# A two-layer encoder trunk on one core: packed first transfer, held transfers, an earlier first norm and one smaller store

## The chip, the core and the metric

The kernel runs on one core of a Trainium2 chip. Its engines are PE (matrix products), ACT and DVE (elementwise work), POOL (a few small operations) and SP (which only issues transfers). The metric is the device time of one execution in microseconds, so less is better. Every engine works through its own instructions strictly in order; a tile framework puts waits on semaphores where one engine needs another's result.

## What is computed

The input is 256 tokens of 2048 features; 16 learned tokens are put in front, so there are L = 272 columns. Layer 0 is differential attention with 8 heads, layer 1 a causal pooling mixer. All products are float32 products made of three products of rounded halves (high x high, high x low, low x high).

```python
def rms_norm(x, g):
    y = xf * lax.rsqrt(jnp.mean(xf * xf, axis=-1, keepdims=True) + RMS_EPS)
    return (y * g.astype(jnp.float32)).astype(x.dtype)
...
for i in range(DEPTH):
    hn = rms_norm(h, pre_norm_g[i])
    if i % N_MIXERS == 0:
        y = diff_attention_mixer(hn, attn_w_in[j], attn_w_out[j], ...)
    else:
        y = pool_mixer(hn, pool_w_in[j], pool_w_group[j], pool_scale[j], pool_w_out[j])
    h = h + rms_norm(y, post_norm_g[i])
return h[:, N_META:]
```

## The kernel before

Activations lie transposed: 2048 features are 16 **feature tiles** (numbered 0 to 15 here) of 128 partitions by 272 tokens. A **chunk** is 128 output columns of a weight matrix for all 16 feature tiles (128 x 2048 numbers, 1 MB). Some 120 chunks stream through the core: SP loads one into `raw` (two buffers), ACT rounds it into `hi`, DVE subtracts to get `lo` (`split`, lines 97 and 98), and PE makes 48 products with it (`mm3`, lines 121 to 123).

**The front** is different, since nothing is there to compute on. The array `first` holds, for every feature tile, the 272 tokens of x and the weights of the first four chunks, 784 numbers per partition. It comes in eleven transfers on SP's queue into `pk`: of tile 0 the first 400 columns (line 209) and the rest (line 210), tiles 1, 2 and 3 alone, then pairs (line 212). The small parameters (gains and such, 70 columns) come in a transfer of their own on ACT's queue into `sp` (line 140). PE first makes products of ones (`busy`, line 136) with nothing but time as their result.

The loop over the feature tiles k does, per tile: ACT rounds the weights (line 236, "cast") and writes x times its gain, rounded (line 240, "scale"); DVE subtracts for the low halves of the weights (line 237) and of x (line 241, `xl`); PE makes 12 products (lines 245 to 247: four chunks, three products each); ACT squares x in place (`square0`, line 230). A square of tile k must wait until DVE has read x of that tile in line 241.

The 16 squared tiles are added up on DVE by halving (`fold`, line 107, and line 261), to `sq0`. The **first norm** (`Norm`, lines 166 to 192) then takes: small products of `sq0` with ones on PE (line 174), mean plus epsilon on DVE (line 179), the power -1/2 on POOL (line 180), a spread onto the columns of a matrix on DVE (line 190), and a product with ones on PE (line 191) that gives every partition the factors. They are needed only after the projections (rows of `rp`, lines 270 and 271), so PE can run ahead of them. Before, the fifth chunk (`pq4`, all 48 products) runs first; the norm's small products and the spread stand within the sixth chunk (`pq5`).

Tiles and pools decide which buffer waits for which; the order within each engine is set by a scheduler from the order in the source and the `issue_after` notes. Behind the front, PE runs chunk after chunk to the end, where the last block of 128 tokens is scaled and stored (`out_store`): the first 512 columns by way of PE and ACT's queue, the rest by DVE in slices, each stored by SP (lines 806 and 808).

Of the kernel before, what the change touches and what calls it, by code (L numbers as in the profile page):

```python
# [43 lines left out]
def trunk(ctx: ExitStack, tc: tile.TileContext, first, hT, xt, small, gpost1, rope, w_in, w_out, p_in, p_grp, p_out, out):  # L44
# [95 lines left out]
    act.dma_start(sp, small)  # L140
    rp = const.tile([P, 2, L], F32, name="rp")
    ident = const.tile([P, P], F32, name="ident")
# [3 lines left out]
    ones = const.tile([P, P], F32, name="ones")  # L146
    pool.memset(ones, 1.0)
    warm = const.tile([P, 1], F32, name="warm")
    act.square(warm, ones[:, 0:1])
# [49 lines left out]
    busy(6)  # L199
# [6 lines left out]
    pk = xp.tile([P, KT, L + NF * P], F32, name="pk")  # L206
# [25 lines left out]
    for k in range(KT):  # L232
        hi, lw = fhi[:, k], flo[k // 8][:, k % 8]
        for i, n in ((0, 1), (1, NF - 1)) if k == 0 else ((0, NF),):
# [3 lines left out]
            if i == 0:  # L238
                g = sp[:, C_PRE0 + k:C_PRE0 + k + 1]
# [32 lines left out]
    run_part(NF + 1, 12, 4)  # L272
# [8 lines left out]

    lp = const.tile([P, 2], F32, name="lp")
    dve.tensor_tensor(out=lp, in0=sp[:, C_LAM:C_LAM + 2], in1=sp[:, C_LAM + 2:C_LAM + 4], op=ALU.mult)
    psl = bank("psl")
    pe.matmul(psl[:, 0:2], ones, lp, start=True, stop=True)
    le = const.tile([P, 2], F32, name="le")
    act.activation(le, psl[:, 0:2], AF.Exp)
    dve.scalar_tensor_tensor(out=lamc, in0=le[:, 0:1], scalar=LAM_INIT, in1=le[:, 1:2], op0=ALU.add, op1=ALU.subtract)
# [221 lines left out]
    for slot in range(NH * 6 + KT):  # L510
# [17 lines left out]
        if slot == NF + 2:  # L528
# [372 lines left out]
```

## Time and profile before

| what | value |
|---|---|
| median of 3 runs | 837.65 us (837.34 to 837.66) |
| profiled execution: time | 837.55 us |
| profiled execution: span, first to last instruction | 835.8 us |
| PE busy | 827.9 us (99%) |
| DVE, ACT busy | 585.4 us (70%), 437.8 us (52%) |
| share of the time to the chain that ended last | PE 98%, transfers 1% |

PE is busy nearly all the time, so what the end depends on is PE's own work and the few stretches in which PE has to wait: the first 8 us, a norm, and the last 8 us. The time of the profiled execution is 1.75 us longer than its span, and lies 0.10 us under the median of the runs.

### The profile page before, as it was taken

What the parts mean: (1) busy time and instruction counts of PE and PEld (TensorE: products, weight loads), DVE (VectorE), ACT (ScalarE), POOL (GpSimd) and SP (SyncE); (2) the same over time, 40 slices, a digit from 0 to 9 for tenths busy, and PEclk for the clock granted to TensorE, in tenths of its full rate; (3) what the DMA queues carried; (4) which work ended last, traced back from release to release, by engine and by line L of the source; (5) the groups of instructions that cost most, each with busy time, mean ns of one, the idle gap of its engine ahead of it and who ended that gap; (6) DMA issues with size and microseconds to landing.
All of it is one profiled execution on the core that took longest, in us unless ns stands there. A gap on an engine that the chain in (4) does not pass through costs nothing.

```text
span 835.8 us, 14454 instructions
## 1 busy us (share of the span) xinstructions
PE 827.9 (99%) x6060; PEld 796.5 (95%) x6060; DVE 585.4 (70%) x960; ACT 437.8 (52%) x680; POOL 3.4 (0%) x13
## 2 busy tenths in 40 slices
PE   9999999999999999999999999999999999999997
PEld 8999999999999999999999999999999888888886
DVE  6799767675868687897854644697998666685523
ACT  8646555454546465855444544654544545563422
POOL 0000000000000000000000000000000000000000
PEclk9999999999999999999999999999999999999999
DMA  9446444444444444355459744146556555545512
GB/s 356 170 151 203 154 153 157 163 164 162 160 152 152 152 151 151 134 175 197 152 193 367 280 174 151 51 162 242 184 195 263 176 191 202 178 174 206 197 51 101
DMA packets 22385, 149.35 MB, mean 179 GB/s; under 512 B 2608, under 2 KB 2992, under 8 KB 5552
## 3 DMA queue, kind: packets, MB, share of 16 engines
q1 hardware_dynamic: 22032, 148.14, 48.7%
q8 instruction: 47, 0.77, 0.4%
q10 hardware_dynamic: 288, 0.30, 0.1%
q14 instruction: 18, 0.15, 0.1%
HBM read 146.33 MB, written 2.10 MB: 178 GB/s over the span
## 4 chain that ended last, share of the span: by engine, by line
PE 98%; DMA 1%; DVE 0%; ACT 0%; issue 0%; SPq 0%; DVEq 0%; ACTq 0%
PE p L121 14%; PE p L123 14%; PE p L122 14%; PE pv L129 7%; PE py L121 4%; PE py L123 4%; PE py L122 4%; PE pu L121 4%; PE pu L122 4%; PE pu L123 4%; PE pv L130 4%; PE pz L772 4%; PE pz L770 4%; PE pz L771 3%; PE pm L129 2%; PE pq L245 1%
## 5 line engine op out<-in xcount | busy, mean ns | idle before, releaser
L98 DVE TENSOR_TENSOR lo<-raw,hi 128x2048 fp32r<-128x2048 f32 (+1 forms) x123 | 279.2, 2270 | 136.4 <-ACT hi L97 135.9
L97 ACT CAST hi<-raw 128x2048 fp32r<-128x2048 f32 (+1 forms) x123 | 232.9, 1895 | 194.0 <-PE p L122 96.2
L121 PE MATMUL p<-xs,hi 128*128 128x272 f32 x928 | 270.2, 291 | 0.0
L123 PE MATMUL p<-xs,lo 128*128 128x272 f32 x928 | 268.4, 289 | 0.0
L122 PE MATMUL p<-xs,hi 128*128 128x272 f32 x928 | 267.5, 288 | 0.0
L121 PEld LDWEIGHTS p<-xs,hi 128*128 128x128 f32 x928 | 174.8, 188 | 0.3
L122 PEld LDWEIGHTS p<-xs,hi 128*128 128x128 f32 x928 | 174.8, 188 | 0.0
L123 PEld LDWEIGHTS p<-xs,lo 128*128 128x128 f32 x928 | 174.6, 188 | 0.0
L129 PE MATMUL pv<-hs,hi 128*128 128x512 f32 x256 | 89.5, 393 | 0.0
L121 PE MATMUL py<-os,hi 128*128 128x272 f32 x256 | 74.3, 290 | 0.0
L123 PE MATMUL py<-os,lo 128*128 128x272 f32 x256 | 74.1, 289 | 0.0
L122 PE MATMUL py<-os,hi 128*128 128x272 f32 x256 | 73.7, 288 | 0.0
L130 PE MATMUL pv<-hs,lo 128*128 128x256 f32 x256 | 71.8, 280 | 0.0
L121 PE MATMUL pu<-hs,hi 128*128 128x260 f32 (+3 forms) x224 | 63.8, 285 | 0.0
L123 PE MATMUL pu<-hs,lo 128*128 128x260 f32 (+3 forms) x224 | 63.7, 285 | 0.0
L122 PE MATMUL pu<-hs,hi 128*128 128x260 f32 (+3 forms) x224 | 63.6, 284 | 0.0
L129 PEld LDWEIGHTS pv<-hs,hi 128*128 128x128 f32 x256 | 48.0, 188 | 10.9
L122 PEld LDWEIGHTS py<-os,hi 128*128 128x128 f32 x256 | 48.3, 189 | 0.0
L121 PEld LDWEIGHTS py<-os,hi 128*128 128x128 f32 x256 | 48.2, 188 | 0.0
L123 PEld LDWEIGHTS py<-os,lo 128*128 128x128 f32 x256 | 48.2, 188 | 0.0
L130 PEld LDWEIGHTS pv<-hs,lo 128*128 128x128 f32 x256 | 48.1, 188 | 0.0
L771 PE MATMUL pz<-lo,zs 128*128 128x512 f32 (+1 forms) x120 | 45.0, 375 | 0.0
(251 smaller groups left out, 1316.9 us busy)
## 6 DMA issues: line engine op xcount, KB each, us to landing
raw<-in_w_in SPq DMA_DIRECT2D x60, 1024.0 KB, 4.8
raw<-in_p_in SPq DMA_DIRECT2D x29, 1024.0 KB, 4.8
raw<-in_w_out SPq DMA_DIRECT2D x16, 1024.0 KB, 4.8
raw<-in_p_out SPq DMA_DIRECT2D x14, 1024.0 KB, 4.8
pk<-in_first SPq DMA_DIRECT2D x6, 784.0 KB, 10.8
raw<-in_p_grp SPq DMA_DIRECT2D x4, 1024.0 KB, 4.9
rawu<-in_p_in SPq DMA_DIRECT2D x3, 1024.0 KB, 5.4
h<-in_hT SPq DMA_DIRECT2D x4, 544.0 KB, 7.2
```

Of the source, the lines that this page charges most:

```text
L97: act.copy(hi[:, s], raw[i][:, s])
L98: rest[i] = dve.tensor_tensor(out=lw[:, s], in0=raw[i][:, s], in1=hi.bitcast(F32)[:, s], op=ALU.subtract)
L121: pe.matmul(o, wh, xh, start=first, stop=False)
L122: pe.matmul(o, wh, xl, start=False, stop=False)
L123: pe.matmul(o, wl, xh, start=False, stop=last)
L129: pe.matmul(ps[:, 0:2 * n], wh, x, start=first, stop=False, skip_group_check=not first)
L130: pe.matmul(ps[:, 0:n], wl, x[:, 0], start=False, stop=last)
L245: pe.matmul(o, hi[:, i], xh[:, k, :], start=k == 0, stop=False)
L770: pe.matmul(ps, zh[:, k, s], wh[:, c], start=k == 0, stop=False)
L771: pe.matmul(ps, zh[:, k, s], wl[:, c], start=False, stop=False)
L772: pe.matmul(ps, zl[:, k, s], wh[:, c], start=False, stop=k == KT - 1)
```

## The change

- The small parameters move into the first columns of `first`, so the first transfer carries 470 columns instead of 400, and ACT's small transfer is gone. POOL copies them to `sp`.
- Before the transfer of feature tile 2 is issued, POOL writes one number into its place, copied from the first transfer's data. So SP's queue waits there until the first transfer has landed and POOL has run; the later transfers stand behind it in SP's order.
- `ones` is set by DVE instead of POOL, and `busy` makes 7 products instead of 6.
- The first norm's products stand in the fifth chunk (after 8 and 13 of its 16 feature tiles); the fold of the second half of the squares goes ahead of the sixth chunk's `lo`; the attention's lambda is computed in the front; the seventh chunk's `split` comes behind the norm, the eighth's halves are made apart.
- The last store's columns 512 to 2048 go out as 256, 512, 512, 256 columns instead of 640, 512, 384.

```diff
-    sp = const.tile([P, C_END], F32, name="sp")
-    act.dma_start(sp, small)
+    ones = const.tile([P, P], F32, name="ones")
+    dve.memset(ones, 1.0)
...
-    busy(6)
+    busy(7)
...
-    nc.sync.dma_start(pk[:, 0, 0:L + P], first[:, 0, 0:L + P])
-    nc.sync.dma_start(pk[:, 0, L + P:], first[:, 0, L + P:])
-    for a, b in ((1, 2), (2, 3), (3, 4), (4, 6), (6, 8), (8, 10), (10, 12), (12, 14), (14, 16)):
-        nc.sync.dma_start(pk[:, a:b, :], first[:, a:b, :])
-    load(NF)
-    nc.sync.dma_start(rp, rope)
+    ends = [0, C_END + L + P] + [C_END + k * (L + NF * P) for k in (1, 2, 3, 4, 6, 8, 10, 12, 14, 16)]
+    for a, b in zip(ends, ends[1:]):
+        if a == ends[3]:
+
+            pool.tensor_copy(pks[:, a:a + 1], pks[:, 0:1])
+        with (tc.issue_after(held.ins) if a > ends[3] else ExitStack()):
+            held = nc.sync.dma_start(pks[:, a:b], first[:, a:b])
+    act.square(warm, ones[:, 0:1])
+    pool.tensor_copy(sp, pks[:, 0:C_END])
+    with tc.issue_after(held.ins):
+        load(NF)
+        nc.sync.dma_start(rp, rope)
...
-    split(NF + 1)
+    fold(s8[:, 8:KT], s8[:, 8])
+    t = dve.tensor_tensor(out=sq0, in0=s8[:, 0], in1=s8[:, 8], op=ALU.add)
+    with tc.issue_after(t.ins):
+        split(NF + 1)
     load(NF + 3)
-    with tc.issue_after(rest[NF + 1].ins):
-        fold(s8[:, 8:KT], s8[:, 8])
-        dve.tensor_tensor(out=sq0, in0=s8[:, 0], in1=s8[:, 8], op=ALU.add)
-    run_part(NF, 0, KT)
-    run_part(NF + 1, 0, 5)
+    run_part(NF, 0, 8)
     norm0 = Norm(sq0, "pre0", rcol0).power()
-    with tc.issue_after(norm0.vi.ins):
-        split(NF + 2)
-    run_part(NF + 1, 5, 7)
-    dve.tensor_copy(r0, norm0.spread(r0))
+    run_part(NF, 8, 5)
+    r0c = dve.tensor_copy(r0, norm0.spread(r0))
...
+    run_part(NF, 13, 3)
+    with tc.issue_after(r0c.ins):
+        split(NF + 2)
...
+    run_part(NF + 1, 0, KT)
...
-        for c in (slice(512, 1152), slice(1152, 1664), slice(1664, D)) if b else (slice(0, 512), slice(512, 1280), slice(1280, D)):
+        for c in (slice(512, 768), slice(768, 1280), slice(1280, 1792), slice(1792, D)) if b else (slice(0, 512), slice(512, 1280), slice(1280, D)):
```

What it does to the order on the engines shows at two places. On **ACT**, feature tiles 1 to 4: a row that reads fhi<-pk 128x512 is the cast of a tile, xs<-pk the scale, pk<-pk the square. Before, from the cast of tile 1 on:

```order
L236 CAST fhi<-pk 128x512
L240 ACTIVATE xs<-pk,sp 128x272
L236 CAST fhi<-pk 128x512
L240 ACTIVATE xs<-pk,sp 128x272
L230 ACTIVATE pk<-pk 128x272
L236 CAST fhi<-pk 128x512
L240 ACTIVATE xs<-pk,sp 128x272
L230 ACTIVATE pk<-pk 128x272 x2
L236 CAST fhi<-pk 128x512
```

After the change, again from the cast of tile 1 to that of tile 4:

```order
L241 CAST fhi<-pk 128x512
L245 ACTIVATE xs<-pk 128x272
L235 ACTIVATE pk<-pk 128x272
L241 CAST fhi<-pk 128x512
L245 ACTIVATE xs<-pk 128x272
L241 CAST fhi<-pk 128x512
L245 ACTIVATE xs<-pk 128x272
L235 ACTIVATE pk<-pk 128x272 x2
L241 CAST fhi<-pk 128x512
```

The square of tile 1 has moved from behind the scale of tile 2 to ahead of the cast of tile 2. PE's order moves within three tiles, too: the 12 products of tile 4 stood in threes of one kind (three of line 245, three of 246, three of 247, then the fourth chunk's), and now stand chunk by chunk, so the third of them already reads the low half `xl` of x.

On **DVE**, from the split of the fifth chunk (lo, in two halves) to the norm's factors (r), before:

```order
L222 TENSOR_TENSOR lo_127<-raw_115,hi_126 128x1024 x2
L98 TENSOR_TENSOR lo_412<-raw_118,hi_411 128x2048
L107 TENSOR_TENSOR pk<-pk 128x4x272
L107 TENSOR_TENSOR pk<-pk 128x2x272
L107 TENSOR_TENSOR pk<-pk 128x272
L261 TENSOR_TENSOR sq_99<-pk 128x272
L179 TENSOR_SCALAR v_pre_488<-rms_pre_484 128x3
L98 TENSOR_TENSOR lo_492<-raw_398,hi_491 128x2048
L190 TENSOR_SCALAR r_87<-ident,rcol_83 128x16
```

After the change:

```order
L227 TENSOR_TENSOR lo_129<-raw_117,hi_128 128x1024 x2
L107 TENSOR_TENSOR pk<-pk 128x4x272
L107 TENSOR_TENSOR pk<-pk 128x2x272
L107 TENSOR_TENSOR pk<-pk 128x272
L263 TENSOR_TENSOR sq_98<-pk 128x272
L98 TENSOR_TENSOR lo_418<-raw_120,hi_417 128x2048
L177 TENSOR_SCALAR v_pre_451<-rms_pre_447 128x3
L188 TENSOR_SCALAR r_85<-ident,rcol_81 128x16
```

The fold and `sq0` now come ahead of the sixth chunk's `lo`, which still stands ahead of the norm's first DVE step; between that step and the factors no split stands any more.

## Rows read from the trace of the kernel before

**Rows 1.** The page's first part: busy time of each engine, share of the span, instructions.
```profile
PE 827.9 (99%) x6060; PEld 796.5 (95%) x6060; DVE 585.4 (70%) x960; ACT 437.8 (52%) x680; POOL 3.4 (0%) x13
```

**Rows 2.** The waits of PE over the whole span: who waited for whom, us in total, times, longest.
```profile
PE pq L245 <- ACT xs L240: 0.8, 2, 0.6
...
PE rms_pre L191 <- DVE r L190: 0.2, 1, 0.2
```

**Rows 3.** The chain of waits in its first stretch, in order of time: start, us, what.
```profile
1.65 4.83 DMA pk<-in_first
...
6.50 0.62 ACT fhi L236
7.12 0.43 ACT xs L240
...
7.60 0.64 PE pq L245 x3
```

**Rows 4.** What the transfers moved in three stretches from the span's start; the last column is GB/s over the stretch.
```profile
0.00:3.43 3.43, 2.30 (x10) 2.30 (x11) 0.06 (x1) 1.49 (x2) 1.13 (x9) 1.00 0.45 129
0.00:5.00 5.00, 3.67 (x15) 3.38 (x16) 1.27 (x6) 2.83 (x6) 1.13 (x9) 1.00 0.58 168
0.00:6.48 6.48, 5.15 (x22) 4.86 (x23) 1.48 (x6) 3.04 (x6) 1.13 (x9) 1.00 0.68 215
```

**Rows 5.** SP's first two issues on the timeline: start, us, line.
```profile
0.74 0.38 SPq L209 DMA_DIRECT2D pk<-in_first  x1
1.17 0.42 SPq L210 DMA_DIRECT2D pk<-in_first  x1
```

**Rows 6.** Transfers by issue: KB each, us from issue to landing. The first two are those of rows 5; the third is of two issues, those of tiles 1 (1.65, in rows 3) and 2 (2.11), with their mean.
```profile
pk<-in_first SPq DMA_DIRECT2D x1, 200.0 KB, 2.7
pk<-in_first SPq DMA_DIRECT2D x1, 192.0 KB, 2.8
pk<-in_first SPq DMA_DIRECT2D x2, 392.0 KB, 5.1
```

**Rows 7.** ACT's timeline, tiles 1 to 4 of the front.
```profile
7.47 0.62 ACT L236 CAST fhi<-pk 128x512 fp32r<-128x512 f32 x1
...
8.74 0.60 ACT L236 CAST fhi<-pk 128x512 fp32r<-128x512 f32 x1
...
10.51 0.43 ACT L230 ACTIVATE pk<-pk 128x272 f32<-128x272 f32 x1 [0.42 <-DVE xs L241]
10.85 0.60 ACT L236 CAST fhi<-pk 128x512 fp32r<-128x512 f32 x1
```

**Rows 8.** DVE's timeline: the low half of x of tile 1 and of tile 4.
```profile
7.76 0.50 DVE L241 SCALAR_TENSOR_TENSOR xs<-pk,sp,xs 128x272 fp32r<-128x272 f32 x1
...
12.10 0.50 DVE L241 SCALAR_TENSOR_TENSOR xs<-pk,sp,xs 128x272 fp32r<-128x272 f32 x1
```

**Rows 9.** PE's timeline: the first product of tile 5, the first of the fifth chunk, the first norm's small products and the second product behind them, the last product ahead of the spread, the spread, and the first product of the seventh chunk.
```profile
13.72 0.29 PE L245 MATMUL pq<-xs,fhi 128*128 128x272 f32 x1
...
30.27 0.28 PE L121 MATMUL pq<-xs,hi 128*128 128x272 f32 x1
...
38.22 0.72 PE L174 MATMUL rms_pre<-ones,sq 128*128 128x1 f32 x6
...
39.01 0.29 PE L122 MATMUL pq<-xs,hi 128*128 128x272 f32 x1
...
41.91 0.29 PE L121 MATMUL pq<-xs,hi 128*128 128x272 f32 x1
42.37 0.73 PE L191 MATMUL rms_pre<-r,ones 128*128 128x272 f32 x2 [0.17 <-DVE r L190]
...
44.07 0.37 PE L121 MATMUL p<-xs,hi 128*128 128x272 f32 x1
```

**Rows 10.** DVE's timeline between the front and the norm: `lo` of the fifth chunk, of the sixth, the fold, `sq0`.
```profile
26.66 2.36 DVE L222 TENSOR_TENSOR lo<-raw,hi 128x1024 fp32r<-128x1024 f32 x2
29.73 2.29 DVE L98 TENSOR_TENSOR lo<-raw,hi 128x2048 fp32r<-128x2048 f32 x1 [0.71 <-ACT hi L97]
31.95 2.52 DVE L107 TENSOR_TENSOR pk<-pk 128x1088 f32<-128x1088 f32 x3
34.50 0.44 DVE L261 TENSOR_TENSOR sq<-pk 128x272 f32<-128x272 f32 x1
```

**Rows 11.** The timeline of layer 1's norm, made of the same steps with no split between them: the small products on PE, the mean on DVE, the power on POOL, the factors on DVE.
```profile
565.93 0.72 PE L174 MATMUL rms_pre<-ones,sq 128*128 128x1 f32 x6
566.69 0.16 DVE L179 TENSOR_SCALAR v_pre<-rms_pre 128x3 f32<-128x3 f32 x1 [2.19 <-PE rms_pre L174]
566.93 0.86 POOL L180 TENSOR_TENSOR r_pre<-v_pre,mhalf 128x3 f32<-128x3 f32 x1 [526.77 <-DVE v_pre L179]
567.82 0.62 DVE L190 TENSOR_SCALAR r<-ident,r_pre 128x16 f32<-128x16 f32 x3 [0.97 <-POOL r_pre L180]
```

**Rows 12.** The end on the timeline: DVE's three slices and SP's three stores of them.
```profile
829.32 2.08 DVE L806 SCALAR_TENSOR_TENSOR ht<-y,rf,ht 128x640 f32<-128x640 f32 x3
...
830.23 1.52 SPq L808 DMA_DIRECT2D out<-ht  x3
```

**Rows 13.** What the transfers moved in two stretches at the end; the last column is GB/s.
```profile
831.00:833.50 2.50, 0.00 (x0) 0.00 (x0) 0.39 (x1) 0.31 (x1) 0.00 (x0) 0.81 1.00 370
833.50:834.00 0.50, 0.00 (x0) 0.00 (x0) 0.00 (x0) 0.00 (x0) 0.00 (x0) 0.50 0.73 247
```

More of the change, by code (lines that the diff above doesn't have):

```diff
@@ L43, in trunk @@
 @with_exitstack
-def trunk(ctx: ExitStack, tc: tile.TileContext, first, hT, xt, small, gpost1, rope, w_in, w_out, p_in, p_grp, p_out, out):
+def trunk(ctx: ExitStack, tc: tile.TileContext, first, hT, xt, gpost1, rope, w_in, w_out, p_in, p_grp, p_out, out):
     nc = tc.nc
@@ L145, in trunk @@
                        base=0, channel_multiplier=1)
-    ones = const.tile([P, P], F32, name="ones")
-    pool.memset(ones, 1.0)
     warm = const.tile([P, 1], F32, name="warm")
-    act.square(warm, ones[:, 0:1])
     ones_r = const.tile([P, P], F32R, name="ones_r")
@@ L238, in trunk @@
             if i == 0:
-                g = sp[:, C_PRE0 + k:C_PRE0 + k + 1]
+                g = pks[:, C_PRE0 + k:C_PRE0 + k + 1]
                 act.activation(xh[:, k, :], pk[:, k, 0:L], AF.Copy, scale=g)
@@ L256, in trunk @@
         square0(k)
-    split(NF + 1)
+    fold(s8[:, 8:KT], s8[:, 8])
+    t = dve.tensor_tensor(out=sq0, in0=s8[:, 0], in1=s8[:, 8], op=ALU.add)
+    with tc.issue_after(t.ins):
+        split(NF + 1)
     load(NF + 3)
-    with tc.issue_after(rest[NF + 1].ins):
-        fold(s8[:, 8:KT], s8[:, 8])
-        dve.tensor_tensor(out=sq0, in0=s8[:, 0], in1=s8[:, 8], op=ALU.add)
-    run_part(NF, 0, KT)
-    run_part(NF + 1, 0, 5)
+    run_part(NF, 0, 8)
     norm0 = Norm(sq0, "pre0", rcol0).power()
-    with tc.issue_after(norm0.vi.ins):
-        split(NF + 2)
-    run_part(NF + 1, 5, 7)
-    dve.tensor_copy(r0, norm0.spread(r0))
+    run_part(NF, 8, 5)
+    r0c = dve.tensor_copy(r0, norm0.spread(r0))
     dve.tensor_tensor(out=rp[:, 0, :], in0=rp[:, 0, :], in1=r0, op=ALU.mult)
     dve.tensor_tensor(out=rp[0:ROPE, 1, :], in0=rp[0:ROPE, 1, :], in1=r0[0:ROPE, :], op=ALU.mult)
-    run_part(NF + 1, 12, 4)
+    lp = const.tile([P, 2], F32, name="lp")
+    dve.tensor_tensor(out=lp, in0=sp[:, C_LAM:C_LAM + 2], in1=sp[:, C_LAM + 2:C_LAM + 4], op=ALU.mult)
+    run_part(NF, 13, 3)
+    with tc.issue_after(r0c.ins):
+        split(NF + 2)
+    psl = bank("psl")
+    pe.matmul(psl[:, 0:2], ones, lp, start=True, stop=True)
+    le = const.tile([P, 2], F32, name="le")
+    act.activation(le, psl[:, 0:2], AF.Exp)
+    dve.scalar_tensor_tensor(out=lamc, in0=le[:, 0:1], scalar=LAM_INIT, in1=le[:, 1:2], op0=ALU.add, op1=ALU.subtract)
+    run_part(NF + 1, 0, KT)
     x0.close()
@@ L279, in trunk @@
     ssb = att.tile([P, NH, L], F32, name="ssb")
[L282 to L288, printed above, removed]
     sub = const.tile([P, 2], F32, name="sub")
@@ L526, in trunk @@
             proj(ps, 0, L, xh, xl)
-        if slot == NF + 2:
+        if slot == 0:
+            i7 = cur[0] + 1
+            load(i7)
+            halves[i7] = (wpool.tile([P, CW], F32R, tag="hi", name=f"hi{i7}"), wpool.tile([P, CW], F32R, tag="lo", name=f"lo{i7}"))
+            act.copy(halves[i7][0], raw[i7])
+        elif slot == NF:
+            rest[i7] = dve.tensor_tensor(out=halves[i7][1], in0=raw[i7], in1=halves[i7][0].bitcast(F32), op=ALU.subtract)
+        elif slot == NF + 2:
             with tc.issue_after(heads[0].done.ins):
@@ L874 @@
     w_in = _tiles(A(attn_w_in)[0])
+    small = np.concatenate([
+        _cols(A(pre_norm_g)[0]), _cols(A(pre_norm_g)[1]), _cols(A(post_norm_g)[0]), _cols(A(pool_scale)[0]),
+        _cols(A(attn_subln_g)[0]), _cols(A(attn_lambda_q1)[0]), _cols(A(attn_lambda_q2)[0]),
+        _cols(A(attn_lambda_k1)[0]), _cols(A(attn_lambda_k2)[0])], axis=1)
     arrays = {
-        "first": np.ascontiguousarray(np.concatenate(
-            [hT] + [w_in[c].reshape(P, KT, P) for c in FIRST], axis=2)),
+        "first": np.ascontiguousarray(np.concatenate([small, np.concatenate(
+            [hT] + [w_in[c].reshape(P, KT, P) for c in FIRST], axis=2).reshape(P, -1)], axis=1)),
         "hT": hT,
         "xt": np.ascontiguousarray(A(x)[0]),
-        "small": np.ascontiguousarray(np.concatenate([
-            _cols(A(pre_norm_g)[0]), _cols(A(pre_norm_g)[1]), _cols(A(post_norm_g)[0]), _cols(A(pool_scale)[0]),
-            _cols(A(attn_subln_g)[0]), _cols(A(attn_lambda_q1)[0]), _cols(A(attn_lambda_q2)[0]),
-            _cols(A(attn_lambda_k1)[0]), _cols(A(attn_lambda_k2)[0])], axis=1)),
         "gpost1": np.ascontiguousarray(A(post_norm_g)[1:2]),
```

3 lines of the change are left out of this document (2 added, 1 removed).

## The prediction

> **What bounds the kernel now.** I read the page's busy times first: PE is busy 827.9 of 835.8 us [rows 1], so the time can only change where PE waits or idles. The list of PE's waits comes second: in the front it waits twice for ACT's scaled tile, 0.8 us together, the longer 0.6, and 0.2 us for the norm's spread [rows 2]. Third, the chain of waits of the first 14 us: it starts at the transfer of feature tile 1, issued at 1.65 and landed 4.83 later, at 6.48; then ACT's cast and scale, and PE's first product of tile 1 at 7.60 [rows 3]. From there PE runs without a gap up to the spread. So the front is set by tile 1's landing, and what the change gives or takes is decided between that landing and the first product of tile 5, at 13.72 [rows 9]; behind it PE is the slowest engine. The rest is the norm's wait and the last stores.
>
> **Tile 1's landing, T.** Before, T = 6.48. Its own bytes and those ahead of it are 200 + 192 + 392 KB and 35 KB of small parameters, 0.84 MB. By 5.00 us 168 GB/s had moved just that much, by 6.48 us 215 GB/s had moved 1.39 MB [rows 4]. So 0.55 MB of later tiles had moved before tile 1 was whole. The hold keeps these out. Bounds: at the high end nothing moves, T = 6.48. At the low end the bytes are through at 5.00, plus the lag with which the second transfer landed: it landed at 1.17 + 2.8 = 3.97 [rows 5, 6], when its bytes and those ahead (0.44 MB) were through at 3.43 (129 GB/s) [rows 4], 0.54 later. That makes 5.54. I take 5.8, since the second transfer is the nearest row, but tile 1 has twice its bytes and may lag half as much again (0.8). The first transfer is 35 KB longer and ACT's transfer of 35 KB is gone: nothing.
>
> **From T to tile 5.** The new order on ACT costs something here. The square of tile 1 now stands ahead of the cast of tile 2, and waits for DVE to read x of tile 1. Before, with T = 6.48, that read ended at 7.76 + 0.50 = 8.26 [rows 8]; the square would start 0.04 later and hold ACT 0.34 (10.51 to 10.85 [rows 7]), so the cast of tile 2 starts at 8.64, T + 2.16, where it stood at 7.47 [rows 7]. To the cast of tile 3 it is one cast and one scale, 0.97 (6.50 to 7.47 [rows 3, 7]). From there to the cast of tile 4 the work is as before less a square that only moves behind a wait for DVE, 10.85 - 8.74 = 2.11 [rows 7]. So the cast of tile 4 starts at T + 5.24; before it was T + 4.37. PE's order adds to it: the third product of tile 4 now needs the low half of x, ready at 12.60 before [rows 8], that is 1.75 after the cast; 0.04 later that product starts, and ten products of 0.125 ((30.27 - 13.72) / 132 [rows 9]) are left until tile 5: 1.79 + 1.25 = 3.04. Tile 5 starts at T + 8.28. With T = 5.8 that is 14.08, against 13.72: **+0.36**. PE's wait ahead of tile 1 goes, and comes back ahead of tiles 2 to 4. From tile 5 on PE stays last (before, DVE was through with the tiles by 26.66 [rows 10], 3.6 us before PE [rows 9]), and the fifth chunk starts at 30.63.
>
> **The held transfers.** Tile 2 was issued at 2.11; now SP waits for the first landing (0.74 + 2.7 = 3.44 [rows 5, 6]), POOL's one-element copy and two semaphores, some 0.25 as an estimate, so about 3.7. All eight issues behind it on SP wait as well, and the chunks' loads. ACT wants tile 2 at T + 2.16 = 7.96, so 4.3 are left. The 392 KB transfers took 4.8 and 5.4 (mean 5.1 [rows 6]), but with 0.5 MB of others in between; the small ones took 2.7 and 2.8. With three transfers' bytes through at about 5.0, tile 2's 0.40 MB at the rate between the two last rows (0.55 MB in 1.48 us [rows 4]) are through near 6.1 and land near 6.9. I count nothing, and keep the other end as a rival.
>
> **The norm.** Before, the last product ahead of the spread started at 41.91 and the spread at 42.37 [rows 9]: 0.46, where products stand 0.125 apart, so 0.33 lost, because DVE's factors stood behind a split. Now no split stands between the mean and the factors; layer 1 has such a norm [rows 11]: from the small products to the factors' end 567.82 + 0.62 - 565.93 = 2.51, plus 0.05 to PE, 2.56. PE's cover is 15 products: 0.79 from the small products to the second product behind (38.22 to 39.01 [rows 9]), and 14 of 0.125: 2.54. So the wait is 0.02; POOL may take 0.1 longer to start, so 0.02 to 0.12. Two things must be in time. The squares' sum: DVE ends the fifth chunk's lo at 29.02 and needs 2.99 for fold and sum [rows 10], so 32.0; PE wants it 24 products into the chunk, at 33.3 or later. And the sixth chunk's lo, which stands ahead of the mean on DVE, holds it 2.2 (29.73 to 31.95 [rows 10]), to 34.2; the mean can start at 33.3 + 0.76 = 34.05 (566.69 - 565.93 [rows 11]). With the front's shift of ACT (+0.2) and of PE (+0.36) the two come out level at 34.4. Saved: 0.33 - 0.07 = **-0.26**.
>
> **The end.** The first slice falls from 640 to 256 columns, so SP's first store of DVE's part goes out some 0.45 us sooner (829.32 to 830.23 for 640 columns [rows 12]). But the stores are bound by what moves: 370 GB/s from 831.0 on, 1.05 MB to the last byte [rows 13]. 128 KB are gone in 0.35 us, and the next slice of 512 columns needs 0.66 (1.52 for three issues [rows 12] with the columns between them), so about 0.3 of the 0.45 is lost as a gap. I take **-0.1**, with bounds 0 and -0.45.
>
> **Nothing** for the rest: the seventh product of ones ends near 4.4, at most 0.2 behind the first scale, and PE still is done with tile 0 before tile 1's scale or within 0.2 of it, while tiles 2 to 4 wait longer than that. The lambda's and copies' small steps on DVE and POOL lie beside waits. Splits of the seventh and eighth chunks come later in DVE's order but are wanted by PE at 44 us and later; the cover is 5 us. The order of PE's instructions behind the seventh chunk is unchanged, and PE does not wait there.
>
> **Sum.** 837.55 (the profiled execution; the runs' median is 0.10 higher) + 0.36 - 0.26 - 0.1 = 837.55, rounded **837.6**. A measurement of this kernel can tell 0.2%, 1.7 us, from no change; none of the terms is that large, for all the gaps of the front together are under 1 us.
>
> **Rivals.** (a) The hold frees nothing: each transfer is limited by the engines that carry it, and what stands behind it in the queue only uses others' idle time. For: the transfers behind had not kept tile 1 from the queue's head. Against: 0.55 MB moved first. Then T = 6.48, tile 5 starts at 14.76, and the sum is 837.55 + 1.04 - 0.26 - 0.1 = 838.2, slower. It decides from T = 5.8, where the terms cancel. The Trainium skill (DMA: Bandwidth & Descriptors, Queues, rings and completion order) states that every DMA engine takes its descriptors in the order of its ring and that a transfer is complete when its last engine is; by that rule what queues behind delays nothing, and the sum is that of this rival. The trace agrees only in part: that later bytes moved first fits engines that run ahead.
> (b) The hold costs a transfer's latency: tile 2, issued at 3.7, takes as long as 392 KB took before, 5.4, and lands at 9.1, behind the 7.96 at which ACT wants it. Then the cast of tile 4 comes at 9.1 + 0.97 + 2.11 = 12.2 and tile 5 at 15.2: +1.5, and 838.7, slower. It decides where issue to landing exceeds 4.3. For: single tiles never took less than 4.8. Against: much less is in flight.
> (c) Little is lost and the end gains all: T at 5.3, tile 5 at 13.58 (-0.14), norm -0.26, stores -0.45: 836.7, faster. For: the second transfer's lag was short; against: T would lie under its own low bound.
>
> **How the numbers follow.** Forecast, 837.2 to 837.9 with T between 5.4 and 6.1: 0.50. (a) 0.22, (b) 0.12, (c) 0.16. The range 836.8 to 838.6 holds the forecast, (a), most of (c) and little of (b). All cases but a tail of (b), where the tiles behind tile 2 are late too, and one of (c) lie within 0.2% of the time before (835.97 to 839.33): faster 0.02, within 0.94, slower 0.04.
>
> **What would show it.** Tile 1's landing in the chain of waits, 5.5 to 6.1 against 6.48; PE without a wait at tile 1 but with waits for ACT or DVE at tiles 2 to 4; ACT waiting for DVE ahead of the square of tile 1; tile 5 near 14.1 and the fifth chunk near 30.6; a wait of 0.1 or less ahead of the spread. I am wrong in the front if ACT waits for tile 2's or 3's transfer (b), or tile 1 lands near 6.5 (a); in the norm if the spread waits over 0.3; wrong as a whole if PE shows a wait behind the seventh chunk's start that it had not before.

## The result and the profile after

| | before | changed |
|---|---|---|
| median of 22 runs each | 837.61 us (837.21 to 837.97) | 838.74 us (838.07 to 839.79) |
| ratio, 95% interval | | 1.0015 (1.0009 to 1.0021) |
| profiled execution: time, span | 837.55, 835.8 | 839.67, 837.9 |

The kernel became slower by 1.13 us in the median and by 2.12 in the profiled execution, which is one of the slower ones: the changed kernel's runs are not one group, most take 838.1 to 838.9 and some 839.2 to 839.8. The prediction was 837.6.

**Busy time and waits.** These answer to [rows 1, 2]. The page's first part:

```profile
PE 829.3 (99%) x6062; PEld 796.5 (95%) x6062; DVE 585.7 (70%) x962; ACT 437.5 (52%) x680; POOL 3.6 (0%) x14
```

PE's waits (who for whom, us in total, times, longest):

```profile
PE pq L250 <- ACT xs L245: 1.0, 2, 0.7
PE po L815 <- ACT diag L813: 0.7, 1, 0.7
PE p L121 <- DVE s L369: 0.7, 1, 0.7
```

The wait ahead of the norm's spread is gone from the list; the wait for `s` in line 369 is new, and lies far behind the front, where I had expected none.

**The front.** The chain of waits in its first stretch (start, us, what), to be held against [rows 3]:

```profile
1.64 4.15 DMA pk<-in_first
5.82 0.63 ACT fhi L241
6.47 0.69 DVE flo L242
7.16 0.42 DVE xs L246
7.61 0.43 ACT pk L235
8.04 0.51 ACT fhi L241
```

Tile 1 landed at 1.64 + 4.15 = 5.79; I had taken 5.8. Then comes what was worked out for the order on ACT: DVE's read of x, the square of tile 1, the cast of tile 2. ACT's timeline has the next steps, and one that was not in the working:

```profile
7.95 0.60 ACT L241 CAST fhi<-pk 128x512 fp32r<-128x512 f32 x1
...
9.88 0.62 ACT L241 CAST fhi<-pk 128x512 fp32r<-128x512 f32 x1 [0.91 <-DMA pk<-in_first]
...
12.01 0.60 ACT L241 CAST fhi<-pk 128x512 fp32r<-128x512 f32 x1
```

The cast of tile 2 starts where it should (T + 2.16 = 7.95). The cast of tile 3 should follow at 8.92 and starts at 9.88, behind a wait for its transfer; the cast of tile 4 then comes 2.13 later, as worked out. The held transfers by issue (KB each, us from issue to landing), tile 2 and tile 3:

```profile
pk<-in_first SPq DMA_DIRECT2D x1, 392.0 KB, 3.9
...
pk<-in_first SPq DMA_DIRECT2D x1, 392.0 KB, 5.8
```

Tile 2, issued at 3.67, landed near 7.57, in time. Tile 3, issued at 4.04, landed near 9.84, 0.92 late. In the kernel before, tile 3 was issued at 2.58 and took as long:

```profile
pk<-in_first SPq DMA_DIRECT2D x1, 392.0 KB, 5.8
```

So the pause of 1.46 in tile 3's issue went through to its landing nearly in full. Which tile comes too late is not the same in every execution. In a second profile of the same kernel (e5 below), tile 2 is late first, and tile 3 a little more; these are the casts of tiles 2 and 3:

```profile
8.50 0.62 ACT L241 CAST fhi<-pk 128x512 fp32r<-128x512 f32 x1 [0.49 <-DMA pk<-in_first]
...
9.71 0.62 ACT L241 CAST fhi<-pk 128x512 fp32r<-128x512 f32 x1 [0.17 <-DMA pk<-in_first]
```

**Behind the front.** PE's timeline, to be held against [rows 9]: the first product of the fifth chunk, the norm's small products, its spread, the first product of the seventh chunk, and of the ninth.

```profile
31.77 0.29 PE L121 MATMUL pq<-xs,hi 128*128 128x272 f32 x1
...
34.79 0.72 PE L172 MATMUL rms_pre<-ones,sq 128*128 128x1 f32 x6
...
37.37 0.73 PE L189 MATMUL rms_pre<-r,ones 128*128 128x272 f32 x2
...
45.33 0.29 PE L121 MATMUL p<-xs,hi 128*128 128x272 f32 x1
...
60.33 0.39 PE L121 MATMUL p<-xs,hi 128*128 128x272 f32 x1 [0.71 <-DVE s L369]
```

In the kernel before, the ninth chunk's row reads

```profile
58.18 0.37 PE L121 MATMUL p<-xs,hi 128*128 128x272 f32 x1
```

So the 2.1 us divide like this. To the fifth chunk: 31.77 against 30.27, +1.50. From there to the seventh: 13.56 against 13.80, -0.24. From there to the ninth: 15.00 against 14.11, +0.89. From there to the end of the span: 777.57 against 777.62, -0.05. Together +2.10.

**The ninth chunk's wait.** DVE's timeline of this stretch: `lo` of the eighth chunk, `lo` of the tenth, and the first reads of the score tile `s` of the first head.

```profile
45.58 2.26 DVE L540 TENSOR_TENSOR lo<-raw,hi 128x2048 fp32r<-128x2048 f32 x1
...
57.18 2.29 DVE L98 TENSOR_TENSOR lo<-raw,hi 128x2048 fp32r<-128x2048 f32 x1 [2.95 <-ACT hi L97]
59.39 0.43 DVE L314 TENSOR_TENSOR qk<-p,rp 128x272 f32<-128x272 f32 x1
59.74 0.15 DVE L368 COPY s<-s 16x16 f32<-16x16 f32 x1
60.19 0.14 DVE L369 TENSOR_TENSOR s<-s,s 16x16 f32<-16x16 f32 x1
```

`lo` of the tenth chunk now stands ahead of the score reads, and its data comes late: SP issues that load when the eighth chunk's `lo` has freed its buffer, at 47.88 (before: 44.54), and here it took long. The load by issue, changed kernel:

```profile
raw<-in_w_in SPq DMA_DIRECT2D x1, 1024.0 KB, 7.3
```

Before, it took

```profile
raw<-in_w_in SPq DMA_DIRECT2D x1, 1024.0 KB, 4.8
```

**The end**, to be held against [rows 12]: DVE's slices and SP's stores.

```profile
831.48 2.21 DVE L819 SCALAR_TENSOR_TENSOR ht<-y,rf,ht 128x256 f32<-128x256 f32 x4
```

```profile
832.00 2.15 SPq L821 DMA_DIRECT2D out<-ht  x4
```

From DVE's first slice to the first store it is 0.52 instead of 0.91, so the store goes out 0.39 sooner; of that, 0.05 is left at the end of the span.

### The profile page after: what moved, and what is told of

It is laid out like the page before. It is cut to its first block, busy times and chain, and to the rows that moved or that the text cites. A ratio compares the mean times of both kernels' runs of the same rounds, so it can differ in the third digit from the quotient of the medians.

```text
span 837.9 us, 14468 instructions
## 1 busy us (share of the span) xinstructions
PE 829.3 (99%) x6062; PEld 796.5 (95%) x6062; DVE 585.7 (70%) x962; ACT 437.5 (52%) x680; POOL 3.6 (0%) x14
## 4 chain that ended last, share of the span: by engine, by line
PE 95%; DVE 2%; DMA 1%; ACT 1%; issue 0%; SPq 0%; DVEq 0%; ACTq 0%
PE p L121 14%; PE p L123 13%; PE p L122 13%; PE pv L129 7%; PE py L121 4%; PE py L123 4%; PE py L122 4%; PE pu L121 4%; PE pu L122 4%; PE pu L123 4%; PE pv L130 4%; PE pz L784 3%; PE pz L783 3%; PE pz L785 3%; PE pm L129 2%; PE pq L252 1%
```

## The experiments

**Theory.** The +1.50 in the front is the held queue: what is issued behind a pause lands later than ACT wants it, above all tile 3. Rivals: the packing; the order on ACT and PE that the scheduler chose together with the hold (the square of tile 1 ahead of the cast of tile 2). For the ninth chunk the theory is the late load with DVE's new order behind it; the rival is chance, or something else that PE waits for.

The runs stand here in groups, by question. This table has them all, by rows of their timelines: starts of ACT's casts of tiles 1, 3 and 4, the start of the fifth chunk on PE, the time from there to the seventh chunk and from the seventh to the ninth, and the median (22 runs of the changed kernel in its first set, 5 of e6, 11 of each other) and ratio to the kernel before, run beside it (before: 837.55 to 837.70 in these sets).

| run | cast 1 | cast 3 | cast 4 | 5th | to 7th | to 9th | median | ratio (95%) |
|---|---|---|---|---|---|---|---|---|
| before | 6.50 | 8.74 | 10.85 | 30.27 | 13.80 | 14.11 | | |
| changed | 5.82 | 9.88 | 12.01 | 31.77 | 13.56 | 15.00 | 838.74 | 1.0015 (1.0009 to 1.0021) |
| e5 changed again | 5.79 | 9.71 | 11.84 | 31.60 | 13.56 | 14.05 | 838.92 | 1.0013 (1.0005 to 1.0022) |
| e1 no hold | 5.88 | 8.88 | 10.99 | 30.27 | 13.44 | 14.16 | 837.60 | 0.9999 (0.9990 to 1.0008) |
| e4 hold later | 6.42 | 8.78 | 10.89 | 30.27 | 13.44 | 14.18 | 837.42 | 0.9999 (0.9990 to 1.0008) |
| e2 hold, old ACT order | 5.75 | 9.77 | 11.90 | 31.65 | 13.56 | 14.59 | 838.75 | 1.0011 (1.0002 to 1.0020) |
| e9 hold of no length | 6.88 | 9.94 | 12.14 | 31.90 | 13.56 | 14.97 | 838.28 | 1.0008 (1.0000 to 1.0017) |
| e10 shorter hold | 6.06 | 9.12 | 11.31 | 31.07 | 13.57 | 14.81 | 838.48 | 1.0010 (1.0001 to 1.0019) |
| e13 no length, late squares | 5.79 | 8.42 | 10.33 | 30.11 | 13.98 | 14.05 | 837.65 | 1.0002 (0.9993 to 1.0011) |
| e14 hold, late squares | 5.79 | 9.57 | 11.51 | 31.25 | 14.02 | 14.05 | 838.96 | 1.0019 (1.0010 to 1.0028) |
| e6 before + hold | 5.55 | 9.87 | 12.00 | 31.68 | 14.21 | 15.20 | 840.62 | 1.0033 (1.0020 to 1.0045) |
| e3 old 7th and 8th chunk | 5.96 | 10.08 | 12.20 | 31.93 | 13.57 | 14.05 | 838.76 | 1.0012 (1.0003 to 1.0021) |
| e7 score reads first | 5.89 | 9.69 | 11.81 | 31.57 | 13.57 | 14.05 | 838.94 | 1.0014 (1.0005 to 1.0023) |
| e8 no hold, late squares | 6.12 | 8.36 | 9.38 | 29.94 | 13.44 | 14.43 | 837.27 | 0.9994 (0.9985 to 1.0003) |
| e11 e8 + e3 | 6.57 | 8.62 | 9.61 | 30.42 | 13.44 | 14.05 | 837.16 | 0.9994 (0.9986 to 1.0003) |
| e12 e8 + e7 | 6.47 | 8.48 | 9.49 | 30.29 | 13.44 | 14.04 | 836.88 | 0.9993 (0.9984 to 1.0001) |

### The hold: taken away, moved, and alone

e1, without the hold:

```diff
-        if a == ends[3]:
-            pool.tensor_copy(pks[:, a:a + 1], pks[:, 0:1])
-        with (tc.issue_after(held.ins) if a > ends[3] else ExitStack()):
-            held = nc.sync.dma_start(pks[:, a:b], first[:, a:b])
+        held = nc.sync.dma_start(pks[:, a:b], first[:, a:b])
```

> The changed kernel without the hold: the twelve transfers of the packed front are issued one behind the other; the norm, the handling of the seventh chunk and the last stores stay as changed. Without the hold the order of ACT's work comes out as before too (the square of tile 1 behind the cast of tile 3). Theory: the 1.50 us by which the fifth chunk starts later in the changed kernel (31.77 against 30.27) is the price of the held queue, above all tile 3 landing at 9.85 where ACT wanted it at 8.92. Then tile 3 lands near 8.4 again, the fifth chunk starts at 30.2 to 30.5, and the median is 837.1 to 837.6, 1.1 to 1.6 below the changed kernel's 838.74. Rival (the packing: the small parameters now ahead of the first columns, the seventh product of ones): the fifth chunk stays at 31.0 or later and the median above 838.3.

The theory held: the whole 1.50 is gone, and the median is that of the kernel before. Tile 1 landed as early as with the hold, and the cast of tile 4 came near where it was before:

```profile
5.88 0.62 ACT L241 CAST fhi<-pk 128x512 fp32r<-128x512 f32 x1 [0.76 <-DMA pk<-in_first]
...
7.60 0.62 ACT L241 CAST fhi<-pk 128x512 fp32r<-128x512 f32 x1 [0.68 <-DMA pk<-in_first]
...
10.65 0.43 ACT L235 ACTIVATE pk<-pk 128x272 f32<-128x272 f32 x1 [0.42 <-DVE xs L246]
10.99 0.60 ACT L241 CAST fhi<-pk 128x512 fp32r<-128x512 f32 x1
```

But this run took back two things at once, since without the hold the scheduler also returns to the old orders.

e4, the hold ahead of the pair of tiles 4 and 5:

```diff
-        if a == ends[3]:
+        if a == ends[5]:
...
-        with (tc.issue_after(held.ins) if a > ends[3] else ExitStack()):
+        with (tc.issue_after(held.ins) if a > ends[5] else ExitStack()):
```

> The changed kernel with the hold two transfers later: tiles 2 and 3 are issued at once, and the pair of tiles 4 and 5 and all behind it wait for the first landing. Theory: what costs is that the first held tiles are wanted sooner than a queue that starts again can land them; tiles 2 and 3 then land at about 7.5 and 8.5, and the pair, issued near 3.8, has until 10.85; it took 7.7 when issued at 4.1 behind two held tiles, and lands near 10.0 to 11.0 here. The fifth chunk starts at 30.2 to 30.9, and the median is 837.2 to 838.0. Rival (each hold costs its latency, wherever it stands): the pair lands at 11.7 or later again, the fifth chunk starts at 31.4 or later, and the median is 838.4 or more.

Here too the fifth chunk starts at 30.27: the rival, that every hold costs its latency, is out. Here a hold is free, since what it delays is wanted late.

e6, the kernel before with the hold alone (a copy on POOL from tile 0's place to tile 2's, and the issues in order):

```diff
+        if a == 2:
+            pool.tensor_copy(pk[:, 2, 0:1], pk[:, 0, 0:1])
...
```

> The kernel before with the hold alone: a one-element copy on POOL, which reads the first piece of tile 0 and writes into tile 2, and SP's issues behind it in order; small parameters on ACT's queue, the norm, the seventh chunk and the last stores stay as before. Theory (the restart of the held queue): tile 3 lands near 9.8 instead of 8.42, the pair behind it near 11.7, the fifth chunk starts at 31.4 to 32.0 instead of 30.27, and the median is 1.1 to 1.7 above that of the kernel before. Rival (the hold costs only together with the packed front): the fifth chunk starts at 30.9 or sooner, and the median is within 0.6 of the kernel before.

The front's +1.41 agrees, the total of +2.97 is larger than either side expected. The rest is lost downstream, at the norm and at the ninth chunk, on PE's timeline:

```profile
44.20 0.72 PE L191 MATMUL rms_pre<-r,ones 128*128 128x272 f32 x2 [0.59 <-DVE r L190]
...
61.09 0.39 PE L121 MATMUL p<-xs,hi 128*128 128x272 f32 x1 [0.83 <-DVE e L396]
```

So the changed kernel's earlier norm spares more with a hold (13.56 to the seventh chunk against 14.21) than without (13.44 against 13.80).

### The hold or the order that came with it

e2, the changed kernel with ACT's square of tile 1 behind the scale of tile 3 (`xa[3]`):

```diff
-        act.square(pk[:, k, 0:L], pk[:, k, 0:L])
+        with (tc.issue_after(xa[3].ins) if k == 1 else ExitStack()):
+            act.square(pk[:, k, 0:L], pk[:, k, 0:L])
```

> The changed kernel with one move on ACT: the square of tile 1 has to stand behind the scale of tile 3, as in the kernel before; DVE's and PE's orders are the changed kernel's, and the hold stays. Theory (late tiles behind the hold): ACT still waits for tile 3 until some 9.85, and then for the pair of tiles 4 and 5, that landed at 11.75; so the cast of tile 4 moves from 12.01 to 11.8 at most, the fifth chunk starts at 31.4 to 31.8, and the median is 838.4 to 838.8. Rival (the order on ACT, that I had counted with 0.87): the cast of tile 4 comes near 11.1, the fifth chunk near 30.9, and the median is 837.9 or less.

As the theory said: the cast of tile 2 comes sooner (7.57), and ACT waits longer for tile 3.

```profile
9.77 0.62 ACT L241 CAST fhi<-pk 128x512 fp32r<-128x512 f32 x1 [1.16 <-DMA pk<-in_first]
```

Under the hold, this move on ACT gains next to nothing (0.12 at the fifth chunk). e9 and e10 ask the reverse, the order without the hold, and with a shorter one. e9 lets the copy read a constant, so it waits for no landing; e10 makes five larger copies of it:

```diff
-            pool.tensor_copy(pks[:, a:a + 1], pks[:, 0:1])
+            pool.tensor_copy(pks[:, a:a + 1], ident[:, 0:1])                          # e9
+            for _ in range(5): pc = pool.tensor_copy(pks[:, a:a + P], ident)           # e10
```

> The changed kernel with the hold's copy on POOL reading a constant instead of the first landed piece; the orders of PE, DVE, ACT and POOL are the changed kernel's, word for word. POOL is through with its constants at 1.55, so the copy is done near 1.7, before SP comes to tile 2 near 2.1: a hold of no length. Theory (what costs is that SP's queue runs dry between 2.1 and 3.7): tile 3 lands at 8.3 to 8.9, ACT casts it at about 8.9, and the fifth chunk starts where the prediction's working for the orders alone puts it, 30.3 to 31.0 (tile 1's landing of 5.8 to 6.2, plus 8.28, plus 16.55); the median is 837.5 to 838.1. Rival (the orders that came with the hold): the fifth chunk starts at 31.5 or later, and the median is 838.5 or more.

> As the run before, with five copies of 128 columns on POOL instead of one: they end near 2.8, so tile 2 is issued near 3.0 instead of 2.1 without a hold and 3.67 in the changed kernel; orders as in the changed kernel, but for POOL's copies. Theory (a dry queue costs about its length): tile 3 lands near 9.2, between 8.5 and 9.85, the fifth chunk starts at 30.8 to 31.4, and the median is 838.0 to 838.5. Rival (each restart of the queue costs a transfer's whole latency, however long the pause): tile 3 lands at 9.7 or later and the fifth chunk starts at 31.5 or later.

e9's median, 838.28, fell between the two ranges: 0.7 above the kernel before, 0.6 below the changed kernel. Its profiled execution has tile 1 late (cast at 6.88), so the fifth chunk's 31.90 can't be read by itself. Counted from the cast of tile 1, the cast of tile 4 comes 5.26 later (e10: 5.25); the prediction had 5.24. In the changed kernel it is 6.19, in the kernel before 4.35. So the order costs 0.9 between these casts, and the hold 0.94 on top. In e10 tile 2 was issued at 3.23 instead of 3.67, tile 3 was in time (cast at 9.12 without a wait), and its median lies between e9's and the changed kernel's. Its fifth chunk, 31.07, is inside the theory's range, but it stands 25.0 behind the cast of tile 1, as e9's does, so tile 1's landing and the order alone give it: this run does not test what a shorter pause costs. What the transfers moved from 4 to 8 us (last column, GB/s), in the changed kernel:

```profile
4.00:8.00 4.00, 2.42 (x7) 1.00 0.82 267
```

in e9:

```profile
4.00:8.00 4.00, 1.96 (x5) 1.00 0.99 351
```

and in e10:

```profile
4.00:8.00 4.00, 2.25 (x6) 1.00 0.90 295
```

The kernel before has 370 there, e1 344 and e5, the changed kernel again, 267. (370 - 267) GB/s over 4 us are 0.41 MB: by 8 us the queue is about one 392 KB tile behind, which fits with one tile being late.

e13 and e14 keep PE's changed order and put ACT's squares of tiles 1 to 3 behind the scale of tile 5, e13 with the hold of no length, e14 with the full one:

```diff
+        with (tc.issue_after(xa[5].ins) if 0 < k < 4 else ExitStack()):
             act.square(pk[:, k, 0:L], pk[:, k, 0:L])
```

> The hold of no length again, with PE's order as in the changed kernel, and ACT's squares of tiles 1 to 3 behind the scale of tile 5. In the two kernels with a short hold, the fifth chunk started 25.04 behind tile 1's landing T, twice; in the kernel before and in those without hold and with late squares, 23.8 to 23.9 behind it. Theory (the square of tile 1, which waits for DVE ahead of tile 2's cast, is this 1.2): the fifth chunk starts at T + 23.7 to T + 24.1, and the median is 837.1 to 837.7. Rival (PE's order of the first tiles, the same here, whose third product of tile 4 needs x's low half): T + 24.7 or more, and the median above 838.0.

> The changed kernel with its full hold and the same late squares. Theory (the late landings of the held tiles bound the front by themselves): tile 3 lands at 9.6 to 9.9 and the pair behind it near 11.7, so the cast of tile 4 comes at 11.6 to 11.9, the fifth chunk starts at 31.3 to 31.8, and the median is 838.3 to 838.8, as in the changed kernel. Rival (the square bounds the front, and the landings only because of what ACT does between them): the fifth chunk starts at 30.9 or sooner, and the median is 837.9 or less.

e13's median is that of the kernel before again (837.65). Its fifth chunk, 24.3 behind tile 1, fell between the ranges. What is left over is lost in tile 2: ACT's cast of it waited 0.62 for its transfer, and PE's second product of the tile starts only when DVE has made the low half of its weights behind that cast, at 8.11 + 0.69 = 8.80:

```profile
7.45 0.62 ACT L241 CAST fhi<-pk 128x512 fp32r<-128x512 f32 x1 [0.62 <-DMA pk<-in_first]
```

```profile
8.11 0.69 DVE L242 TENSOR_TENSOR flo<-pk,fhi 128x512 fp32r<-128x512 f32 x1 [0.42 <-ACT fhi L241]
```

```profile
8.55 0.40 PE L250 MATMUL pq<-xs,fhi 128*128 128x272 f32 x1
8.85 0.39 PE L251 MATMUL pq<-xs,flo 128*128 128x272 f32 x1
```

From 9.50 on PE's products stand 0.125 apart, so e13's wait ahead of the cast of tile 4 does not reach PE. e14 shows the hold by itself: each cast waits for its transfer, and the fifth chunk is 1.14 later than in e13 with nothing else changed. Its 31.25 and 838.96 lie just outside the ranges expected, the first below and the second above, and far from the rival's. The casts of tile 4, of e13:

```profile
10.33 0.62 ACT L241 CAST fhi<-pk 128x512 fp32r<-128x512 f32 x1 [0.86 <-DMA pk<-in_first]
```

and of e14:

```profile
11.51 0.62 ACT L241 CAST fhi<-pk 128x512 fp32r<-128x512 f32 x1 [0.89 <-DMA pk<-in_first]
```

From the cast of tile 4 to the fifth chunk it is 19.73 to 19.78 in all runs with the changed PE order and the hold's code (19.68 in e6, where the hold alone brings that order of tile 4 too), and 19.28 to 19.42 with the old one (before, e1, e4): PE's order itself costs the other 0.3. In e13, where PE did not wait at tile 4, the agreement is chance. In both runs the late squares gave 0.4 back at the norm (13.98 and 14.02 instead of 13.56).

### The ninth chunk

e3 handles the seventh and eighth chunks as before, e7 puts the tenth chunk's `lo` behind the score reads, e5 is the changed kernel as it stands.

```diff
-        if slot == 0:                       # e3: the old code of the slots
-            i7 = cur[0] + 1
...
-        elif slot == NF:
-            rest[i7] = dve.tensor_tensor(out=halves[i7][1], ...)
-        elif slot == NF + 2:
+        if slot == NF + 2:
```

```diff
-            scores(heads[0], lambda: split(cur[0] + 1))      # e7
+            def mid():
+                with tc.issue_after(heads[0].s0r.ins): split(cur[0] + 1)
+            scores(heads[0], mid)
```

In the texts of e3, e11 and e12, "the seventh chunk's halves" are those of the chunk that is called the eighth here, and "the load of the ninth chunk" in e3's is that of the tenth.

> The changed kernel with the seventh chunk's halves handled as before: its low half stands on DVE ahead of the second q/k evacuations instead of behind them, so SP can issue the load of the ninth chunk some 3 us sooner (44.5 instead of 47.88); front, hold, norm and last stores stay as changed. Theory: the wait of 0.7 ahead of chunk nine (first product 15.00 behind the seventh chunk's start instead of 14.11) comes from that load, issued late, that in some runs takes 7.3 us instead of 4.8; with the early load it is gone, the runs at 839.2 to 839.8 are gone, and the median is 838.3 to 838.7. Rival (DVE's order in the first head, that stays the same here, or the chance of the load alone): the runs above 839.2 stay, about one in three, and the wait ahead of chunk nine is seen again when the profile falls in one of them.

> The changed kernel with DVE's low half of the tenth chunk put behind the reads of the first head's score tile, where it stood before; the load of that chunk is still issued late, at about 47.9, behind the low half of the eighth. Theory (the wait of 0.7 ahead of chunk nine is the bank that these reads free, and they wait on DVE behind a low half whose data comes late): chunk nine starts 14.0 to 14.2 behind the seventh chunk as before, whenever the load lands; no run above 839.1. Rival (chunk nine waits for something else, for its own halves or PE's order): its first product comes 14.5 to 15.0 behind the seventh chunk's again in some profile or the runs above 839.1 are as many as in the changed kernel beside it.

> The changed kernel again, as it stands, beside the next three on one chip. In its first runs, about one in three took 839.2 to 839.8 and the others 838.1 to 838.9; the two kernels with a hold that ran beside others on another chip showed nothing above 839.1. Theory (the load of the tenth chunk, issued late, is caught by other traffic in some runs): the high group is there again, at least two of eleven runs above 839.1, and the median is 838.5 to 839.0. Rival (the high group belongs to the chip of the first runs): none above 839.1.

In the profiles nothing speaks against the theory. SP issues the load at 45.35 in e3. Of the kernels with the hold's code and the changed slots, four of seven profiled executions show the wait ahead of the ninth chunk (the changed kernel's 0.71, e9 0.68, e10 0.52, e2 0.29), and e5, e13 and e14 don't. It goes with how long that load takes: 7.3, 7.2, 7.1 and 6.9 us in the four with the wait, in that order, and 6.0, 4.7 and 5.7 in the three without. With either remedy the ninth chunk starts 14.04 or 14.05 behind the seventh in all four (e3, e7, e11, e12), in e7 behind a load of 6.0. In e9's row the releaser is the same:

```profile
60.43 0.40 PE L121 MATMUL p<-xs,hi 128*128 128x272 f32 x1 [0.68 <-DVE s L369]
```

For the times it is open. The runs above 839.2 came again in e5 (two of eleven) and e14 (five of eleven) and not in e3 (none of eleven), but e2, without a remedy, has none either, and e7 has two above 839.1 (839.11 and 839.72), as many as e5 beside it: there the times go with its rival. The medians of e3, e5 and e7 lie within 0.18 of each other, e3's a little above the range expected. That the changed kernel's runs above 839.2 are those with this wait is so for its two profiled executions (839.67 with it, 838.50 without); for the others it is argued, not shown.

### Towards a version that beats both

e8 is e1 with tiles 4 and 5 as two transfers and the late squares of e13; e11 adds e3's code, e12 that of e7.

```diff
-    ... for k in (1, 2, 3, 4, 6, 8, 10, 12, 14, 16)]
+    ... for k in (1, 2, 3, 4, 5, 6, 8, 10, 12, 14, 16)]
```

> The changed kernel without the hold, with tiles 4 and 5 as two transfers, and with ACT's squares of tiles 1 to 3 put behind the scale of tile 5. In the kernel without the hold, tile 1's first product came 0.62 sooner than before (6.98 against 7.60), yet the fifth chunk started at 30.27 as before, because the cast of tile 4 came at 10.99, behind the pair's landing and a square that waited 0.42 for DVE. Theory: with tile 4 landing near 9.5 and no square ahead of its cast, that cast comes near 9.7, PE goes on at its own pace from tile 2 on, and the fifth chunk starts at 29.6 to 30.0; the median is 836.9 to 837.5, 0.5 to 0.9 below the kernel before, which makes it faster than both. Rival (PE's pace from tile 5 on is set by something else, as DVE's halves or the sum of squares): the fifth chunk stays at 30.2 or later, or what is won is lost at the norm's spread, and the median is that of the kernel without the hold, 837.3 to 837.8.

> The kernel without the hold, with single transfers of tiles 4 and 5 and late squares (fifth chunk at 29.94, seventh at 43.38, chunk nine 14.43 behind it instead of 14.1), and with the seventh chunk's halves handled as before, so that the tenth chunk's load can be issued sooner. Theory (the 0.3 lost ahead of chunk nine there is again the tenth chunk's load, which does not come sooner than SP may issue it): chunk nine starts 14.0 to 14.2 behind the seventh, and the median is 836.6 to 837.1, below both kernels. Rival (the load comes no sooner, or chunk nine waits for another thing): chunk nine stays at 14.4 behind the seventh, and the median at 837.2 to 837.5.

> The same kernel without the hold and with late squares, the seventh chunk's halves as in the change, but DVE's low half of the tenth chunk behind the reads of the first head's score tile. Theory (the bank that these reads free): chunk nine starts 14.0 to 14.2 behind the seventh chunk, and the median is 836.6 to 837.1. Rival (the low half itself is the bound, whichever order): what is won at chunk nine is lost at the tenth, and the median stays at 837.2 to 837.5.

e8's front won 0.33 (29.94), and 0.3 of it went at the ninth chunk. e11 and e12 mend that. But the front's gain is tile 1's landing alone: counted from the cast of tile 1, the fifth chunk stands 23.8 behind it in e8, e11 and e12 as in the kernel before, and in e11 and e12, where tile 1 came at 6.57 and 6.47, it starts at 30.42 and 30.29. What their profiles keep is the norm's 0.36. Their medians are 0.4 and 0.7 below the kernel before, the lowest of all, e11's a little above the range expected, yet each interval still holds 1. In its profiled execution (837.85, the longest of its eleven), e12 lost 0.8 behind the ninth chunk (778.33 to the end instead of 777.5); where, was not followed up.

## Why the prediction was wrong

**The step that failed: "The held transfers. [...] I count nothing."** I checked the first held tile alone, tile 2, against the moment when ACT wants it, found a margin and stopped; the passage itself says that all eight issues behind wait as well. Tile 2, issued at 3.67 where 3.7 was worked out, was in time in the first profile. Tile 3 was the one that decided, 0.92 late, and with it +0.94 between the casts of tiles 1 and 4; e10, where no tile is late, and e14 against e13 show this as the hold's own price. In e5's profile tile 2 itself is 0.58 late and tile 3 another 0.2, together +0.80 between the same casts. I had estimated that tile 2 lands 3.2 after its issue, with the rate of a full queue. It took 3.9 (4.7 in e5), and tile 3 took 5.8, as long as in the kernel before; from 4 to 8 us the transfers moved 267 GB/s instead of 370.

**Term by term**, for the profiled execution (the last three rows are differences to the kernel before):

| term | predicted | measured |
|---|---|---|
| tile 1's landing T | 5.8 | 5.79 |
| T to the cast of tile 4, order on ACT | 5.24 | 6.22; 5.26 and 5.25 from cast to cast without late tiles (e9, e10) |
| cast of tile 4 to the fifth chunk | 3.04 + 16.55 = 19.59 | 19.76 |
| fifth chunk | 30.63 (+0.36) | 31.77 (+1.50) |
| norm | -0.26 | -0.24 |
| behind the seventh chunk, ahead of the ninth | 0 | +0.89, and -0.06 in e5 |
| end | -0.1 | -0.05 |

The 1.14 by which the fifth chunk was missed is 0.94 for tile 3, 0.04 for the casts, and 0.17 for PE's order, less 0.01 at T. Against the kernel before, its +1.50 is -0.68 at the cast of tile 1, +0.91 for the order on ACT, +0.94 for the late tile and +0.34 for PE's order, rounded. The first profile is not the typical run: e5's, with +1.33 to the fifth chunk, -0.24 at the norm and no wait ahead of the ninth chunk, took 838.50, nearer to the median of 838.74. So the front, less what the norm saves, makes up most of the median's +1.13. The norm was right in mechanism and size: the spread waits no longer, and stands 2.58 behind the small products, where 2.56 was worked out. In the five kernels without a hold ahead of tiles 2 and 3 and with the old order on PE (e1, e4, e8, e11, e12) it saved 0.36. The end's -0.1 was about right: the stretch from the ninth chunk on is 777.45 to 777.61 in the thirteen profiles with the new stores, e12's aside, against 777.62.

One sign that was named did not show: PE still waited 0.69 ahead of tile 1 (first product 6.92), since it was done with tile 0 sooner than before (last product started at 5.94 instead of 6.75). That cost nothing, since tile 1's landing sets the start.

**"PE does not wait there"**, behind the seventh chunk, failed too. I looked at whether the seventh and eighth chunks' halves would be in time; they were. I did not follow the buffer that the eighth frees: its later `lo` makes SP issue the tenth chunk's load 3.3 us later, and DVE's order had put that chunk's `lo` ahead of the reads that free PE's bank. The prediction named "a wait behind the seventh chunk's start that it had not before" as the sign that it is wrong as a whole.

**The rivals.** (b) came closest: 838.7 was its time, with tile 2 at 9.1; the mechanism was its (issue to landing as long as before), one tile further on, and its chance of 0.12 was too small. That its time is met so closely is partly luck: its 1.1 at tile 2 is, in the first profile, 0.94 at tile 3 and 0.17 more for PE's order. (a), that the hold frees nothing, is not borne out on average. The cast of tile 1 starts at 5.55 to 5.96 in the seven profiles with the full hold, and at 5.79 to 6.88 in the eight where nothing is held ahead of tiles 2 and 3: means 5.79 and 6.33, so with the hold tile 1 comes 0.5 us sooner on average, though e1 and e13 got the same landing without it. The Trainium skill (DMA: Bandwidth & Descriptors, Queues, rings and completion order) states that each DMA engine takes its descriptors in ring order. If that alone decided, the two means would be equal; the trace agrees in e1 (5.88) and e13 (5.79) and not in the means. (c), the gain at the end, did not come: the store went out 0.39 sooner, and 0.05 was left.

## What to carry to other kernels

Where a queue is held, work out the landing of every transfer behind the hold until one has slack of its own, not only of the first: the pause shifts them all, and the one with the least slack sets the price. A hold that begins where the consumer has microseconds to spare (e4) cost nothing here; one that begins at the transfer wanted next cost 0.9 us between ACT's casts (1.14 at the fifth chunk in e14 against e13) and, in the kernel before with its later norm, 3.0 in the median (e6). A hold also changes the order that the scheduler chooses on other engines, and that alone cost 0.9 us between the same casts (e9, e10): compare the orders before reading the times. And where a change moves a split, follow the buffer it frees to the next load, and that load's consumer to whatever stands behind it on its engine.

## What was not expected of the hardware

A queue that is issued to after a pause moved less for several microseconds: from 4 to 8 us 267 GB/s with tile 2 issued at 3.67 (267 again in e5, 278 in e14), 295 with 3.23, and 344 to 370 with no pause (e1, e9, e13, before). Why is open.

The tenth chunk's 1 MB load took 4.8 us in the kernel before, 7.3 in the changed one and 6.0 in its second profile. In the changed kernel 1.02 MB had moved between 48.0 and 53.0, and the load landed at 55.2: the time was lost on its last packets. In the microsecond around its issue the two longer ones list one packet of instructions and no data, the short one data and no instructions. Over all sixteen profiles the two go together, but not strictly: with that packet the load took 5.7 to 7.3 in seven and 4.7 in e13, without it 4.7 to 5.4 in the other eight. It was not tested as a cause. The queue's row in the changed kernel (packets, MB, share):

```profile
q8 instruction: 1, 0.02, 8.6%
```

The landing of the same tile 1, with nothing held, was spread over 1.1 us from kernel to kernel (casts from 5.79 to 6.88).
